# Channel-major projections of a hybrid decoder layer: TensorE in written order, small products in the middle of a later projection

## The chip, the cores and the metric

The kernel runs on one core of one Trainium2 chip. The time is the device time of one execution in microseconds (us), taken as the median of three executions. Lower is better.

## The reference, cut to what matters

One decoder layer over 2048 tokens of width 1024. The part that the change touches is the input projection `z = rms_norm(x) @ w_in` for the column groups that are kept with channels on the partitions, and what hangs on them:

```
z = rms_norm(x, norm_mix) @ w_in
# group A, gated linear recurrence
xc = causal_dwconv(xr, conv_w) + conv_b
r, i = sigmoid(xc @ w_gates[0] + b0), sigmoid(xc @ w_gates[1] + b1)      # block diagonal, 256 channels
a = exp(log_a);  b = sqrt(-expm1(2*log_a)) * (i * xc);  h = scan(a, b)
y_a = h * gelu(gate)
# group B, short convolution
y_b = bg * causal_dwconv(cg * xs)
# group D, compression of keys and of values: blocks of 32 tokens
kc = rms_norm(gelu(einsum('bnld,ldm->bnm', blocks, w1)) @ w2);  vc = the same without the norm
...
mixed = concat(rms_norm(y_a), rms_norm(y_b), rms_norm(y_c), rms_norm(y_d))
```

Attention, the output projection and the feed-forward part follow and are the larger part of the time; the change does not touch them.

## The kernel before

The normalised input lies in SBUF, transposed and split into a high and a low part (`xh`, `xl`, four blocks of 512 tokens). A projection takes one group of 128 weight columns and one block of 512 tokens: 8 slices of the depth, three matmuls each (`mm3`, lines 215 to 217), 24 matmuls into one PSUM tile `z` (pool of 5). There are 44 projections; the text numbers them 0 to 43 in the order of the list `steps`:

- 0 to 3: compression input (`cmp_block`)
- 4 to 7 and 8 to 11: recurrence input, the two halves of the channels (`lrux_block`)
- 12 to 19: the recurrence's gate, both halves in turn (`lrug_block`)
- 20 to 35: short convolution inputs; 36 to 43: its output gate (`scb_block`)

Each projection has a follow-up `fn`, which reads `z` and works on ScalarE (ACT), VectorE (DVE) and GpSimd (POOL). Some follow-ups need small matmuls of their own ("small products"), which are put on the list `later`:

- **gate products** (lines 677 and 679, eight pairs, `ms<-xc,wg`): the r and i gates of the recurrence for the block of one projection of 4 to 11. They need `xc`: two ACT instructions on `z` (667, 670), then three DVE instructions (672).
- Behind a pair of gate products comes a chain: sigmoid r and i, tanh (683 to 685, ACT), 1 + tanh (689, DVE), reciprocal (690, DVE), product (691, DVE), square root (692, ACT), product and scan (693, 694, DVE). Exp (686) is on ACT, a product (687) on POOL.
- **ones products** (line 505, eight times four): sums of squares for the output norm; the last half of the channels only.
- **compression products** (lines 560, 570, 582): 32 products with the compression weights `w1`, which SP loads in four pieces of 512 KB into the buffers of the projection weights, then two with `w2` and a transpose, with a gelu between.
- **decay products** (609, 610): two, for the forget gate's cumulative sum.

In the loop over `steps` the list is run (`drain`) after a projection is written and before its own follow-up; what a follow-up puts on the list is thus written behind the next projection. This is only the order in which the program is written: in this stage a scheduler of the framework orders every engine's queue by its own estimates. TensorE's rows therefore show small products inside later projections, where the scheduler found room. Each queue then runs strictly in its order. In the same stage the scheduler also places 16 `wo_prep` pieces: a load by SP, a cast on ACT (519), a subtraction on POOL (520), a store by SP; one buffer, so that each waits for the store of the one before.

Of the kernel before, what the change touches and what calls it, by code (L numbers as in the profile page):

```python
# [22 lines left out]
KD = D // 128  # L23
# [149 lines left out]
def kernel(ctx, tc, x, norm_mix, w_in, lru_conv_w, lru_conv_b, lru_w_gates, lru_b_gates,  # L173
# [40 lines left out]
    def mm3(ps, ah, al, bh, bl, start, stop):  # L214
        PE.matmul(ps, ah, bh, start=start, stop=False)  # L215
        PE.matmul(ps, ah, bl, start=False, stop=False)  # L216
        PE.matmul(ps, al, bh, start=False, stop=stop)  # L217
# [27 lines left out]
    with ExitStack() as A:  # L245
# [33 lines left out]
        with ExitStack() as A1:  # L279
# [154 lines left out]
            later = []  # L434
            for g, done in ((0, qk_done), (1, qk_done), (2, v_done)):
                for t in range(NT):
# [3 lines left out]
                    z = rows(g, t)  # L440
# [24 lines left out]
        with ExitStack() as A2:  # L465
# [6 lines left out]
            later = []  # L472
            full = {}
            state = {}

            def drain():
                todo = later[:]
                del later[:]
                for fn in todo:
                    fn()  # L480

            def newfull(name):
                full[name] = tm.tile([128, T], F32, name="full", tag="full")
# [2 lines left out]
            def proj(w, j):  # L486
                z = psz.tile([128, 512], F32, name="z")
                for k in range(KD):
                    mm3(z, w[0][:, k, :], w[1][:, k, :], xh[j][:, k], xl[j][:, k], k == 0, k == KD - 1)
                return z  # L490

# [3 lines left out]
            def y_out(g, c, j, y, sq):  # L495

                ACT.activation(sq, y, AF.Square)
                if c:
                    DVE.tensor_add(sq, sq, state["sq"])
                state["sq"] = sq  # L500

                def sums():
                    ms = psm.tile([128, 4, 4], F32, name="ms")
                    for i in range(4):
                        PE.matmul(ms[:, i], sq[:, i * 128:(i + 1) * 128], onec, start=True, stop=True)
                    dst = ssg[:, 4 * j:4 * j + 4, g, 0:1]
                    DVE.tensor_copy(dst, ms[:, :, 0:1])
                if c:
                    later.append(sums)
                k = 2 * g + c  # L510
                hl = tm.tile([128, 2, 512], F32R, name="hl")
                ACT.activation(hl[:, 0], y, AF.Copy, scale=col(R_ON + k))
                DVE.scalar_tensor_tensor(hl[:, 1], y, col(R_ON + k), f(hl[:, 0]), op0=OP.mult, op1=OP.subtract)
                (ACT if g else SP).dma_start(m_d[k, :, :, j * 512:(j + 1) * 512].rearrange("a p t -> p a t"), f(hl))
# [8 lines left out]
            def cmp_block(arg, z, j):  # L523
                if j == 0:
                    for i in range(2):
                        newfull(f"g{i}")
                for i in range(2):
                    zv = z[i * 64:(i + 1) * 64, :].rearrange("p (m e o) -> p e m o", e=8, o=2)
                    gv = full[f"g{i}"].rearrange("p (j n) -> p j n", n=128)
                    for o in range(2):  # L530
                        g = gv[o * 64:(o + 1) * 64]
                        m0 = 1 if j == 0 else 0
                        ACT.copy(g[:, 0:8, 32 * j:32 * j + 32], zv[:, :, :, o])
                        DVE.tensor_copy(g[:, 8:16, 32 * j - 1 + m0:32 * j + 31], zv[:, :, m0:, o])
                if j == 3:
                    later.append(compress)

            def gelu(dst, v, tmp):

# [7 lines left out]
            def compress():  # L547
                for i in range(2):
                    p0 = R_POS + 16 * i
                    gv = full[f"g{i}"].rearrange("p (j n) -> p j n", n=128)  # L550
                    DVE.tensor_copy(gv[:, :, 127], prm[:, p0:p0 + 16])
                    w2 = t1.tile([128, 64], F32, name="w2")
                    SP.dma_start(w2, nsa_cmp_w2[0, i])
                    hp = psk.tile([128, 512], F32, name="kps")
                    for hf in range(2):
                        w1 = wr.tile([128, KD, 128], F32, name="w1", tag="wraw")
                        SP.dma_start(w1, nsa_cmp_w1[0, i, 16 * hf:16 * hf + 16].rearrange(
                            "(j a) d m -> (a d) j m", a=2))
                        for jj in range(8):
                            PE.matmul(hp[:, :128], w1[:, jj, :], gv[:, 8 * hf + jj, :], start=jj + hf == 0,  # L560
                                      stop=jj + hf == 8)
                    hid = t1.tile([128, 128], F32, name="hid")
                    pc = t1.tile([128, 1], F32, name="pc")
                    DVE.tensor_copy(pc, hp[:, 127:128])
                    DVE.tensor_scalar(hid, hp[:, :128], pc, None, op0=OP.add)
                    hg = t1.tile([128, 128], F32, name="hg")
                    ht = t1.tile([128, 128], F32, name="ht")
                    gelu(hg, hid, ht)
                    op = psk.tile([128, 512], F32, name="kps")
                    PE.matmul(op[:, :64], hg, w2, start=True, stop=True)  # L570
                    if i:
                        ACT.copy(vcp[:, 0:64], op[:, :64])
                        DVE.tensor_sub(vcp[:, 64:128], op[:, :64], f(vcp[:, 0:64]))
                        continue
                    k2 = t1.tile([128, 2, 64], F32, name="k2")
                    ss = t1.tile([128, 3], F32, name="ss")
                    ACT.activation(k2[:, 0], op[:, :64], AF.Square, accum_out=ss[:, 0:1])
                    rstd(ss[:, 2:3], ss[:, 0:1], ss[:, 1:2], 1.0 / 64)
                    for a in range(2):
                        DVE.tensor_scalar(k2[:, a], op[:, :64], ss[:, 2:3], None, op0=OP.mult)  # L580
                    kt = psk.tile([128, 512], F32, name="kps")
                    PE.transpose(kt[:, :128], k2.rearrange("p a d -> p (a d)"), ident)
                    ktf = t1.tile([128, 128], F32, name="ktf")
                    kth = t1.tile([128, 128], F32R, name="kth")
                    DVE.tensor_scalar(ktf, kt[:, :128], col(R_KC), None, op0=OP.mult)
                    ACT.copy(kth, ktf)
                    DVE.memset(f(kcp), 0.0)
                    DVE.tensor_copy(kcp[0:64, 0:128], ktf[0:64])
                    DVE.tensor_sub(kcp[64:128, 0:128], ktf[64:128], f(kth[64:128]))

            def fox_decay():
# [16 lines left out]
                def sums():  # L608
# [6 lines left out]
                        DVE.tensor_tensor_scan(s[:, h, 1:NT], z[:, h, 1:NT], a[:, h, 0:NT - 1], 0.0, op0=OP.mult,  # L615
                                               op1=OP.add)
                    DVE.tensor_add(ccol, cp[:, 0:64].rearrange("p (h t) -> p h t", t=NT), s)
                later.append(sums)

            wg = t1.tile([128, 2, 2, 128], F32, name="wg")  # L620

# [133 lines left out]
            for ui, j in steps:  # L755
# [12 lines left out]
                        raws[ui + 3] = wload(wr, "wraw", ui + 3)  # L768
                if ui > 4 and wos:
                    wo_prep(*wos.pop(0))  # L770
                drain()
                fn(arg, z, j)
            drain()
            drain()
    if stop == "A":
        return dict(qk=qk_d, v=v_d, ccol=ccol, gates=gates, kcp=kcp, vcp=vcp)

# [1158 lines left out]
```

## Time and profile before

| what | value |
|---|---|
| median of 3 runs | 2719.72 us (2716.41 to 2719.79) |
| the profiled execution's own time | 2719.14 us |
| its span, first to last instruction | 2717.4 us |
| TensorE busy in the span | 2620.9 us (96%) |
| VectorE / ScalarE / GpSimd busy | 1751.0 (64%) / 1334.6 (49%) / 971.9 us (36%) |
| mean granted TensorE clock | 0.992 of full speed |

"Busy" counts an instruction from its start to its end. Matmuls are pipelined: they start about 0.23 us apart while each is shown as 0.39 us long, so a stage is timed here by starts. The channel-major projections run from about 279 to 582 us of the span.

### The profile page before, as it was taken

The page shows a single profiled execution, that of the slowest core. Times are in us where ns is not written, and L with a number is a line of the kernel's source. Part 1 is how long each engine was busy: PE and PEld are TensorE (multiplying, and loading weights), DVE is VectorE, ACT ScalarE, POOL GpSimd, SP SyncE. Part 2 cuts the span into 40 slices and gives each one's busy share as a digit, 9 for nine tenths or more (in the row PEclk, how much of TensorE's full clock was granted, in tenths as well). Part 3 has the DMA queues.
Part 4 walks back from the last instruction along what each step waited for, and adds up shares of the span by engine and source line. Part 5 has one row for each costly group of instructions (what it writes and reads, how often), then busy time and mean ns, then how long its engine had stood idle before and what let it go on. Part 6 is the DMA issues. An engine that isn't in the chain of part 4 may idle for free.

```text
span 2717.4 us, 39589 instructions
## 1 busy us (share of the span) xinstructions
PE 2620.9 (96%) x13483; PEld 2209.1 (81%) x13483; DVE 1751.0 (64%) x3823; ACT 1334.6 (49%) x2909; POOL 971.9 (36%) x1044
## 2 busy tenths in 40 slices
PE   7999988999988999999999999998999999999999
PEld 5899767889987988888877888887888888888887
DVE  5763487358899999886777666667666555333333
ACT  5431475149987888885444333234333323333331
POOL 1101125114566557750225433433431123224440
PEclk9999999999999999999999999999999999999999
DMA  5444313263432111046765544544543235664553
GB/s 166 121 112 115 118 59 134 77 188 94 110 81 76 50 46 40 25 156 218 247 209 163 175 147 145 169 155 159 178 144 119 75 117 179 211 194 128 184 182 104
DMA packets 314809, 364.73 MB, mean 134 GB/s; under 512 B 25504, under 2 KB 214127, under 8 KB 313839
## 3 DMA queue, kind: packets, MB, share of 16 engines
q1 hardware_dynamic: 312430, 358.02, 42.6%
q10 hardware_dynamic: 2176, 4.19, 0.4%
q8 instruction: 106, 1.74, 0.3%
q14 instruction: 97, 0.79, 0.1%
HBM read 240.24 MB, written 121.90 MB: 133 GB/s over the span
## 4 chain that ended last, share of the span: by engine, by line
PE 56%; DVE 3%; issue 1%; DMA 1%; ACT 1%; POOL 1%; SPq 0%; DVEq 0%; POOLq 0%; ACTq 0%
PE gu L1754 10%; PE gu L1755 10%; PE gu L1753 10%; PE d L1883 5%; PE d L1884 5%; PE d L1882 5%; PE px L215 2%; PE px L217 2%; PE px L216 2%; PE obank L1137 2%; PE tp L1115 1%; PE S L1045 1%; PE S L1046 1%; DMA xraw<-xf_d 1%; DVE P L1060 1%
## 5 line engine op out<-in xcount | busy, mean ns | idle before, releaser
L1753 PE MATMUL gu<-xh,g 128*128 128x512 f32 x1232 | 488.6, 397 | 7.9 <-DVE gq L1715 4.1
L1754 PE MATMUL gu<-xh,g 128*128 128x512 f32 x1232 | 488.6, 397 | 1.4 <-POOL g L1540 1.4
L1755 PE MATMUL gu<-xl,g 128*128 128x512 f32 x1232 | 487.9, 396 | 1.7 <-DVE xl L1663 1.7
L1540 POOL TENSOR_TENSOR g<-guraw,g 128x512 fp32r<-128x512 f32 x136 | 185.8, 1388 | 522.3 <-ACT g L1539 512.6
L1813 DVE TENSOR_TENSOR a<-araw,a 128x512 fp32r<-128x512 f32 x150 | 117.4, 784 | 268.6 <-ACT a L1812 268.6
L1753 PEld LDWEIGHTS gu<-xh,g 128*128 128x128 f32 x1232 | 233.1, 189 | 63.4 <-issue 5.0
L1755 PEld LDWEIGHTS gu<-xl,g 128*128 128x128 f32 x1232 | 233.2, 189 | 56.6 <-DVE xl L1663 2.5
L1754 PEld LDWEIGHTS gu<-xh,g 128*128 128x128 f32 x1232 | 233.0, 189 | 55.7 <-POOL g L1540 2.0
L925 POOL TENSOR_TENSOR pl<-pf,ph 128x512 fp32r<-128x512 f32 x179 | 230.3, 1294 | 111.7 <-ACT ph L911 48.6
L1082 ACT ACTIVATE P<-P,mn 128x1024 f32<-128x1024 f32 (+7 forms) x256 | 225.4, 888 | 20.8 <-DVE mn L1060 20.4
L1883 PE MATMUL d<-b,a 128*128 128x512 f32 x584 | 231.3, 396 | 0.0
L1884 PE MATMUL d<-b,a 128*128 128x512 f32 x584 | 231.2, 396 | 0.0
L1882 PE MATMUL d<-b,a 128*128 128x512 f32 x584 | 231.2, 396 | 0.0
L1812 ACT CAST a<-araw 128x512 fp32r<-128x512 f32 x150 | 93.0, 621 | 279.2 <-PE d L1884 265.7
L1137 PE MATMUL obank<-ph,v 128*128 128x256 f32 (+1 forms) x744 | 197.3, 292 | 3.6 <-ACT ob L962 3.1
L1115 PE MATMUL tp<-ident,P 128*128 128x128 f32 x1368 | 196.7, 274 | 1.2 <-DVE t L975 0.9
L1045 PE MATMUL S<-k,q 128*128 128x512 f32 (+2 forms) x432 | 174.4, 405 | 22.1 <-DVE mn L1060 18.9
L1137 PE MATMUL obank<-pl,v 128*128 128x256 f32 (+1 forms) x744 | 185.4, 283 | 4.2 <-POOL pl L925 2.1
L1115 PEld LDWEIGHTS tp<-ident,P 128*128 128x128 f32 x1368 | 160.0, 142 | 12.5 <-DVE t L975 1.2
L1824 POOL TENSOR_TENSOR b<-braw,b 128x512 fp32r<-128x512 f32 x73 | 102.3, 1414 | 182.7 <-ACT b L1823 181.1
L1046 PE MATMUL S<-k,q 128*128 128x512 f32 (+2 forms) x432 | 152.1, 353 | 0.0
L1539 ACT CAST g<-guraw 128x512 fp32r<-128x512 f32 x228 | 129.7, 617 | 42.6 <-DVE guraw L1610 35.0
(512 smaller groups left out, 6266.6 us busy)
## 6 DMA issues: line engine op xcount, KB each, us to landing
guraw<-in_w_gate_up_dram SPq DMA_DIRECT2D x88, 512.0 KB
araw<-hf_d SPq DMA_DIRECT2D x150, 256.0 KB
hf_d<-uq SPq DMA_DIRECT2D x88, 256.0 KB
q<-qk_d SPq DMA_DIRECT2D x80, 256.0 KB
hf_d<-gq SPq DMA_DIRECT2D x66, 256.0 KB
xt<-in_x_dram SPq DMA_DIRECT2D x32, 512.0 KB
xraw<-xf_d SPq DMA_DIRECT2D x24, 512.0 KB
dnraw<-in_w_down_dram SPq DMA_DIRECT2D x44, 256.0 KB
```

Of the source, the lines that this page charges most:

```text
L925: POOL.tensor_sub(tp["pl"], tp["pf"], f(tp["ph"]))
L1045: PE.matmul(dst, u["q"].tile[:, 0, qs], ks, start=True, stop=False)
L1082: ACT.activation(t, t, AF.Exp, bias=c["mn", a][:, n:n + 1], scale=-1.0, accum_out=c["sum"][:, x, a:a + 1])
L1115: PE.transpose(tp["tp"][:, si, a * 128:(a + 1) * 128], c["P", a, kt // 8][:, kt % 8 * 128:(kt % 8 + 1) * 128], ident)
L1137: PE.matmul(c["o"][:, cs], u["v"].tile[:, kt, :], tp[x][:, si, cs], start=gi == 0 and i == 0, stop=last and i == len(todo) - 1, skip_group ...
L1540: sub.tensor_sub(to[:, 1], src, f(to[:, 0]))
L1753: PE.matmul(p, wh[:, k], xh[:, k], start=j < 4 and k == 0, stop=False, skip_group_check=True)
L1754: PE.matmul(p, wl[:, k], xh[:, k], start=False, stop=False, skip_group_check=True)
L1755: PE.matmul(p, wh[:, k], xl[:, k], start=False, stop=k == HK - 1, skip_group_check=True)
L1882: PE.matmul(p, a[0][:, ts], w[0], start=first, stop=False, skip_group_check=True)
L1883: PE.matmul(p, a[0][:, ts], w[1], start=False, stop=False, skip_group_check=True)
L1884: PE.matmul(p, a[1][:, ts], w[0], start=False, stop=stop_, skip_group_check=True)
```

## The change

Three things change. TensorE's queue in this stage is no longer ordered by the scheduler: it runs in the order in which the program is written. `drain` is called inside a projection, after 12 of its 24 matmuls. And the list has a second level, `after`: what stands there moves to `later` at one drain and runs at the next. Ones products and decay products go to `after`; gate products stay in `later`. The compression becomes a generator that is advanced by one stage at each drain, with its loads of `w1` one stage ahead of the products.

```
@@ A2, before the projections
+            A2.enter_context(tc.manual_schedule(engines={mybir.EngineType.PE}))
+            after, stages = [], []
+
             def drain():
                 todo = later[:]
-                del later[:]
+                later[:] = after[:]
+                del after[:]
                 for fn in todo:
                     fn()
+                if stages:
+                    try:
+                        next(stages[0])
+                    except StopIteration:
+                        stages.pop(0)
@@ proj
                 for k in range(KD):
+                    if k == KD // 2:
+                        drain()
                     mm3(z, w[0][:, k, :], w[1][:, k, :], xh[j][:, k], xl[j][:, k], k == 0, k == KD - 1)
@@ y_out (ones products), fox_decay (decay products)
-                    later.append(sums)
+                    after.append(sums)
@@ cmp_block
-                    later.append(compress)
+                    stages.append(compress())
@@ compress: a yield before each group of eight w1 products, two before the w2 product, one before the transpose
+                        yield
                         for jj in range(8):
                             PE.matmul(hp[:, :128], w1[:, jj, :], gv[:, 8 * hf + jj, :], start=jj + hf == 0,
...
+                    yield
+                    yield
                     op = psk.tile([128, 512], F32, name="kps")
...
+                    yield
                     kt = psk.tile([128, 512], F32, name="kps")
@@ the loop over steps
-                drain()
                 fn(arg, z, j)
-            drain()
-            drain()
+            while later or after or stages:
+                drain()
```

TensorE's queue, projections 4 to 6 of the kernel before (`xh_127` and `xl_128` are the first block of tokens, `xh_129` the second, `xh_131` the third): the first pair of gate products, which belongs to projection 4, stands behind the whole of projection 5, with a compression product between.

```order
L215 MATMUL z<-xh_129,wh_2548 128x512
L216 MATMUL z<-xl_130,wh_2548 128x512
L217 MATMUL z<-xh_129,wl_2550 128x512
L677 MATMUL ms<-xc,wg 128x512
L570 MATMUL kps<-w_2919,hg 128x64
L679 MATMUL ms<-xc,wg 128x512
L215 MATMUL z<-xh_131,wh_2548 128x512
```

The same pair in the changed kernel (its lines 692 and 694 are 677 and 679 of before, 572 is 560): it stands in the middle of projection 5, with the first eight `w1` products behind it.

```order
L215 MATMUL z<-xh_129,wh_2548 128x512
L216 MATMUL z<-xl_130,wh_2548 128x512
L217 MATMUL z<-xh_129,wl_2550 128x512
L692 MATMUL ms<-xc,wg 128x512
L694 MATMUL ms<-xc,wg 128x512
L572 MATMUL kps<-full,w_2912 128x128 x8
L215 MATMUL z<-xh_129,wh_2548 128x512
```

What moved: every pair of gate products now stands half a projection behind the projection that it belongs to. Counted through the whole queue, the eight pairs stood in the middle or at the start of projections 6, 7, 9, 9, 12, 12, 15 and 15 (the last one after 367 of the 1056 projection matmuls); now they stand in the middle of 5 to 12 (the last one after 300). The compression products stand in 5, 6, 8, 9, 10, 11 and 13, the ones products in 16, 18, 20, 22, 40 and 42 and, the last two groups, at the end.

VectorE's queue late in the recurrence inputs, before: two blocks' chains (689 to 694) are worked in pairs, with the `xc` instructions (672) of two later projections behind one another.

```order
L691 TENSOR_TENSOR it<-it,lrc 128x512
L689 TENSOR_SCALAR lrc<-it 128x512
L690 RECIPROCAL lrc<-lrc 128x512
L693 TENSOR_TENSOR it<-it 128x512
L691 TENSOR_TENSOR it<-it,lrc 128x512
L694 SCALAR_TENSOR_TENSOR full<-lr,full,it 128x512
L672 SCALAR_TENSOR_TENSOR xc<-xr,prm,xc 128x512 x4
L693 TENSOR_TENSOR it<-it 128x512
```

The same queue of the changed kernel at the seventh and eighth block (704 to 709 are 689 to 694 of before, 687 is 672, 576 to 577 are 564 to 565, the start of the compression's second gelu):

```order
L704 TENSOR_SCALAR lrc<-it 128x512
L705 RECIPROCAL lrc<-lrc 128x512
L687 SCALAR_TENSOR_TENSOR xc<-xr,prm,xc 128x512
L706 TENSOR_TENSOR it<-it,lrc 128x512
L687 SCALAR_TENSOR_TENSOR xc<-xr,prm,xc 128x512
L681 COPY xr<-xr 128x3
L687 SCALAR_TENSOR_TENSOR xc<-xr,prm,xc 128x512
L708 TENSOR_TENSOR it<-it 128x512
L709 SCALAR_TENSOR_TENSOR full<-lr,it 128x512
L576 COPY pc<-kps 128x1
L709 SCALAR_TENSOR_TENSOR full<-lr,full,it 128x512
L577 TENSOR_SCALAR hid<-kps,pc 128x128
```

What moved: one block's chain at a time, and the `xc` of the next block stands behind the reciprocal of the block before it; two scans and the compression's first instructions stand ahead of the next chain.

GpSimd's queue in the recurrence inputs, one piece of the difference (702 is 687 of before, 531 is 520, the subtraction of `wo_prep`):

```order
-L687 TENSOR_TENSOR it<-it,xc 128x512 x2
-L520 TENSOR_TENSOR wo<-wo 128x512
-L687 TENSOR_TENSOR it<-it,xc 128x512 x2
+L702 TENSOR_TENSOR it<-it,xc 128x512
+L531 TENSOR_TENSOR wo<-wo 128x512
+L702 TENSOR_TENSOR it<-it,xc 128x512
+L531 TENSOR_TENSOR wo<-wo 128x512 x2
+L702 TENSOR_TENSOR it<-it,xc 128x512
```

What moved: one or two `wo` subtractions now stand between every two blocks of the recurrence; before, three ran in this stretch.

## Rows read from the trace of the kernel before

**Rows 1.** Windows: from, to, length, busy of PE, PEld, DVE, ACT, POOL
```profile
311.00:404.00 93.00, 82.19 (x354) 61.09 (x354) 69.51 (x87) 65.11 (x87) 20.43 (x14) 0.98 0.26 83
```

**Rows 2.** Waits of PE, 278 to 582 us: total us, times, longest
```profile
PE ms L505 <- DVE gt L499: 4.9, 3, 2.0
PE ms L677 <- issue: 4.1, 1, 4.1
PE kps L560 <- DMA w<-in_nsa_cmp_w_dram: 2.8, 3, 1.9
PE kps L609 <- DVE fe L602: 2.8, 1, 2.8
PE kps L570 <- DVE hg L545: 1.9, 1, 1.9
PE ms L677 <- DVE xc L672: 1.9, 1, 1.9
PE ms L505 <- DVE tt L719: 1.6, 1, 1.6
PE z L215 <- DVE gg L700: 1.3, 1, 1.3
```

**Rows 3.** Timeline of PE, undisturbed projections: start, length (us); 399 matmuls later
```profile
464.16 0.39 PE L217 MATMUL z<-xh,wl 128*128 128x512 f32 x1
...
554.64 0.39 PE L217 MATMUL z<-xh,wl 128*128 128x512 f32 x1
```

**Rows 4.** Timeline of PE behind the decay products; 10 matmuls later
```profile
294.01 0.63 PE L216 MATMUL z<-xl,wh 128*128 128x512 f32 x1
...
298.27 0.63 PE L217 MATMUL z<-xh,wl 128*128 128x512 f32 x1
```

**Rows 5.** Timeline: projection 4's end, its xc, first and last gate product
```profile
312.18 0.39 PE L217 MATMUL z<-xh,wl 128*128 128x512 f32 x1
...
313.91 2.33 DVE L672 SCALAR_TENSOR_TENSOR xc<-xr,prm,xc 128x512 f32<-128x512 f32 x3 [0.51 <-ACT xc L670]
...
324.35 1.02 PE L677 MATMUL ms<-xc,wg 128*128 128x512 f32 x2
...
402.84 1.02 PE L677 MATMUL ms<-xc,wg 128*128 128x512 f32 x2
```

**Rows 6.** Timeline: instructions of the chain, from several blocks
```profile
399.63 1.12 PE L677 MATMUL ms<-xc,wg 128*128 128x512 f32 x2 [1.89 <-DVE xc L672]
402.30 0.71 ACT L685 ACTIVATE it<-lr,lcoef 128x512 f32<-128x512 f32 x1
...
381.25 1.00 DVE L689 TENSOR_SCALAR lrc<-it 128x512 f32<-128x512 f32 x1 [2.45 <-ACT it L685]
382.29 3.35 DVE L690 RECIPROCAL lrc<-lrc 128x512 f32<-128x512 f32 x1
385.68 0.69 DVE L691 TENSOR_TENSOR it<-it,lrc 128x512 f32<-128x512 f32 x1
...
350.08 1.40 DVE L672 SCALAR_TENSOR_TENSOR xc<-xr,prm,xc 128x512 f32<-128x512 f32 x2
```

**Rows 7.** Groups of instructions in 311 to 404 us: count, busy us, mean ns
```profile
L692 ACT ACT_TABLE_LOAD x6 | 7.7, 1283 | 0.1
...
L694 DVE TENSOR_TENSOR_SCAN full<-lr,full,it 128x512 f32<-128x512 f32 x4 | 5.1, 1272 | 0.0
```

**Rows 8.** Timeline: a POOL subtraction and a DVE product beside it
```profile
372.62 2.78 POOL L271 TENSOR_TENSOR wl<-wraw,wh 128x1024 fp32r<-128x1024 f32 x1
...
373.13 2.82 DVE L693 TENSOR_TENSOR it<-it 128x512 f32<-128x512 f32 x1
```

**Rows 9.** Timeline: a gate product behind the longest stall, and its tanh
```profile
376.71 1.40 PE L677 MATMUL ms<-xc,wg 128*128 128x512 f32 x2 [4.13 <-issue]
...
380.50 0.71 ACT L685 ACTIVATE it<-lr,lcoef 128x512 f32<-128x512 f32 x1
```

**Rows 10.** Timeline: the first of the last two groups of ones products
```profile
578.43 0.95 PE L505 MATMUL ms<-onec,sqy 128*128 128x4 f32 x8
```

More of the change, by code (lines that the diff above doesn't have):

```diff
@@ L617, in sums @@
                     DVE.tensor_add(ccol, cp[:, 0:64].rearrange("p (h t) -> p h t", t=NT), s)
-                later.append(sums)
+                after.append(sums)
             wg = t1.tile([128, 2, 2, 128], F32, name="wg")
@@ L770 @@
                     wo_prep(*wos.pop(0))
+                fn(arg, z, j)
+            while later or after or stages:
                 drain()
-                fn(arg, z, j)
-            drain()
-            drain()
     if stop == "A":
```

## The prediction

> **What bounds the kernel now.** I looked first at the busy table: TensorE is busy 96% of the span, so a change of its order can only win back its stalls and the time at half clock, stage by stage. The stage is the channel-major projections, 279 to 582 us. There are 44 x 24 = 1056 projection matmuls; undisturbed they start 90.48 / 399 = 0.2268 us apart [rows 3], so they need 239.5 of the 303 us. The rest is small products, waits and half clock. The table of waits [rows 2] shows which: eight entries, together 21.3 us; another, 1.5 us at the very end, stays in place. That is what could be won, plus some half clock: behind the 2.8 us wait for the decay products matmuls start 4.26 / 10 = 0.426 us apart [rows 4], which is 1.2 of the 2.4 GHz.
>
> Then I asked who is late. In 311 to 404 us, the recurrence inputs, TensorE was busy 82 of 93 us, VectorE 70 and ScalarE 65 [rows 1]. The last gate product started at 402.84, the first at 324.35 [rows 5]: seven blocks in 78.5 us, 11.2 each, while a projection with its pair of gate products needs only 24 x 0.2268 + 1.3 = 6.7 us of TensorE. So the pace here is that of the chain on VectorE and ScalarE; TensorE filled the time with later projections and had issued 367 matmuls when the last pair came. The changed order allows it 300.
>
> **The change, part by part.**
>
> *The start.* The decay products come a projection and a half later, where their input is long there. This saves the wait of 2.8, 10 x (0.426 - 0.227) = 2.0 us of half clock and some 0.7 around it: 5.5 us. Projection 4's last matmul thus starts at 312.18 - 5.5 = 306.7. Its `xc` was ready 313.91 + 2.33 - 312.18 = 4.1 us after that start [rows 5], so 310.8; half a projection is 2.7 us, so TensorE waits 1.4 us there. Before, this pair stood behind the whole next projection and the first compression products, at 324.35: the chain begins 13.5 us sooner.
>
> *The chain, per block.* After the start of a gate product its tanh ends 402.30 + 0.71 - 399.63 = 3.4 us later; then 1.00 (add), 3.35 (reciprocal), and, in the new order of VectorE, one `xc` instruction, the product (0.69) and two more `xc` instructions (1.40 for two, so 0.70 for one) [rows 6], with 0.2 for a copy and hand-overs. The next gate product waits for the last of these: 3.4 + 1.0 + 3.35 + 0.7 + 0.69 + 1.4 + 0.2 = 10.7 us. TensorE cannot shorten this, and it can no longer run past: it has 6.7 us of work per block, 8.5 with eight `w1` products, so it idles 2 to 4 us in each. Seven blocks: 74.9 us.
>
> *What stands in the chain's way.* (a) The compression's VectorE and ScalarE work now lies inside five of the seven intervals. The queues show ahead of the next link: gelu pieces of 0.2 to 0.4 us, another table load for the tanh and one for the square root (1.28 each), one scan in front of `xc` (1.27) and, at the seventh block, two [rows 7]. Some of it hides beside the reciprocal. I take 9 us; all hidden would be 0, all in line about 12. (b) A `wo` subtraction on GpSimd now falls between every two blocks, just when VectorE has its products to do. Beside a GpSimd subtraction of 2.78 us a VectorE product of 0.69 us ended after 2.82, 0.55 us after GpSimd's end [rows 6, 8]: it was held. A subtraction of 128x512 is half that long, so up to 1.4 per block; I take 4 us for seven blocks, with 0 and 7 as bounds. The Trainium skill (SBUF — State Buffer, "Who interferes with whom") has it as an exclusive lock: a VectorE instruction with two SBUF inputs blocks for the whole GpSimd instruction. By that rule the upper bound would be the better value; the rows agree where the two start together, but not every block will.
>
> (c) Half clock. Behind the 4.1 us stall a gate product took 1.40 instead of 1.12 us, and its tanh ended 380.50 + 0.71 - 376.71 = 4.5 us after its start instead of 3.4 [rows 6, 9]. The stalls of 2.8 and 4.1 us were followed by half clock, those of 1.9 us were not [rows 2, 4, 9]. By the sums above, idling is 2 to 3 us in three of the seven intervals and over 4 in the others. I take 1.1 us in three or four of them, 4 us; 0 and 8 are the bounds.
>
> *The last gate product* then starts at 310.8 + 74.9 + 9 + 4 + 4 = 402.7, which is where it was (402.84); but 67 matmuls fewer are done, 15.2 us.
>
> *What is behind it.* The pair takes 1.3 us. Then come 756 x 0.2268 = 171.5 us of projections, six groups of ones products at about 1.0 [rows 10], 0.7 for the last compression product and restarts: 402.7 + 1.3 + 171.5 + 6.0 + 0.7 = 582.2 for the start of the last two groups. Before, that start was at 578.4 [rows 10]: 402.84 + 1.3 + 689 x 0.2268 = 156.3, + 6.0, + the waits of 4.9 + 1.6 + 1.3 [rows 2], and the remaining 4 us restarts and half clock. Those 7.8 us of waits go, and the 4 with them, because a group now stands two projections behind its `later` piece, 10.9 us, where it stood one behind. I leave 1.2 us of them (bounds 0 and 6.5), since the weight casts of projections 20 and 24 and the bias table now stand in front of the last blocks' work on ScalarE and GpSimd. Sum: 582.2 + 1.2 - 578.4 = +5.0.
>
> The other engines' rows outside the stage and what follows it are unchanged; the tail of the stage too. The waits for `w1` (2.8) vanish, because each piece is asked for a stage ahead, hidden behind at least 10 us of chain against some 4 us of loading; they are in the sum by the first gate's time.
>
> On the profiled execution's 2719.14 us this gives 2724.1; I say **2724**. It is 0.16% above the median of 2719.72, so inside the 0.2% (5.4 us) that I take as what a measurement can tell from no change.
>
> **The rivals.**
>
> 1. *Faster: the pieces hide.* Compression, `wo` and clock cost next to nothing, because the reciprocal (3.35) and the table loads leave holes for them. Then the last gate product starts near 310.8 + 74.9 + 3 = 388.7, and the sum becomes 5.0 - 14 = -9: 2710. For it: VectorE was busy only 70 of 93 us [rows 1]. Against: the queues are strict, and the pieces stand in front of the link, not beside it.
>
> 2. *Clearly slower: every gate at half clock.* Each of the seven pairs costs 1.1 us, (a) and (b) are at their upper ends: + 4 + 3 + 3, and 2 us of half clock behind the last pair: 5.0 + 12 = +17, 2736. The table [rows 2] speaks for it as far as idle stretches over 2.8 us are concerned. It decides against the kernel when the last gate product starts later than about 403.1. The Trainium skill (TensorE: Matmul & The Clock Gate, "Why this matters for your kernels") speaks against this change: it advises against idle gaps between bursts of matmuls, because the clock falls back to half. By it nearly all of the seven would be slow; here stalls of 1.9 us were not.
>
> 3. *Nothing changes,* because this stage's pace is VectorE's and ScalarE's whatever TensorE does: what is won at the start and at the ones products is lost at the gates. This is my forecast but for its size; the sum leans by 5 us to the slow side.
>
> 4. *The ones products still wait.* If ScalarE's casts hold the gate blocks' gelu up, the 6.5 us of waits stay: 2729. A part of the slower case.
>
> **How the numbers follow.** Within 0.2%: 0.43, the likeliest, around 2724 (the forecast, with rival 3). Slower by more: 0.39 (0.29 for rival 2 and for any two of (a) to (c) above what I took, 0.10 for rival 4). Faster by more: 0.18 (rival 1). The range reaches to both: from 2710 (rival 1) to 2735 (nearly rival 2); I leave 1 in 10 on either side. The likeliest case's own range is 2715 to 2725.
>
> **What would show it.** After: gate products waiting for `xc` in nearly all eight places, together 25 to 35 us, where it was 6 [rows 2]; no waits for the decay products, `w1` and the ones products; first gate product near 311, last near 403; intervals of 11 to 15 us; more windows at half clock between 311 and 404. The prediction is wrong if the last gate product starts before 392 (the pieces hide) or after 410 (the lock, the clock or a late `wo` load that holds ScalarE's queue cost more than I took), or if ones products wait over 3 us in all.

## Result and profile after

The changed kernel takes **2741.53 us** (median of 5, 2738.64 to 2746.84) against 2719.72 us (median of 5): ratio **1.0079, 95% interval 1.0069 to 1.009**, slower by some 21.5 us. The forecast was 2724 and the range 2710 to 2735; the time lies above it. The profiled execution took 2738.64 us, 19.5 more than the profiled one of before, with a span of 2736.9. In the changed kernel's file the lines of the stage are 11 to 15 higher: the gate products are 692 and 694, the `xc` instructions 687, add, reciprocal, product 704 to 706, the scan 709, the ones products 516, the `w1` products 572, the `wo` cast and subtraction 530 and 531.

First TensorE's waits from 278 to 606 us, to set beside [rows 2] (total us, times, longest):

```profile
PE ms L692 <- DVE xc L687: 27.2, 7, 7.7
PE ms L692 <- issue: 6.5, 1, 6.5
PE ms L516 <- DVE gt L510: 4.9, 2, 3.5
PE ms L516 <- DVE sqy L510: 1.5, 1, 1.5
PE z L217 <- POOL wl L271: 0.8, 1, 0.8
```

All eight gate pairs wait, 33.7 us in all. The waits for the decay products, for `w1` and for the compression's gelu (`hg`) are gone, and those of the ones products fell from 6.5 to 4.9. Without the 1.5 us at the end, which stayed, TensorE stalls 39.4 us where it stalled 21.3.

Then the places, from the timeline of TensorE (start, duration, and in brackets the wait ahead):

```profile
312.81 1.12 PE L692 MATMUL ms<-xc,wg 128*128 128x512 f32 x2 [2.82 <-DVE xc L687]
...
383.98 1.10 PE L692 MATMUL ms<-xc,wg 128*128 128x512 f32 x2 [3.39 <-DVE xc L687]
...
394.78 1.10 PE L692 MATMUL ms<-xc,wg 128*128 128x512 f32 x2 [1.57 <-DVE xc L687]
...
411.70 2.05 PE L692 MATMUL ms<-xc,wg 128*128 128x512 f32 x2 [7.71 <-DVE xc L687]
413.54 1.91 PE L694 MATMUL ms<-xc,wg 128*128 128x512 f32 x2
...
479.52 1.03 PE L516 MATMUL ms<-onec,gt 128*128 128x4 f32 x8 [3.52 <-DVE gt L510]
```

The eight pairs start at 312.81, 326.30, 341.13, 355.36, 370.90, 383.98, 394.78 and 411.70: intervals of 13.5, 14.8, 14.2, 15.5, 13.1, 10.8 and 16.9, 98.9 us together (before 78.5, [rows 5]). The pairs at 341, 355, 371 and 412 ran at half clock, 2.02 to 2.05 instead of 1.10 us for the two matmuls of a first product; at 313 and 326 only the second product was slow (1.83 and 1.63 instead of 1.02), and the pairs at 384 and 395 were not slow at all. The last two groups of ones products start at 600.88 instead of 578.43 [rows 10]; the layer's later parts give 3 us back.

Who kept the pairs waiting? The waits of VectorE in the same stretch, and two places of its timeline:

```profile
DVE lrc L704 <- ACT it L700: 17.7, 7, 4.8
...
DVE full L709 <- PE kps L572: 8.3, 2, 5.0
```

```profile
326.07 0.68 DVE L708 TENSOR_TENSOR it<-it 128x512 f32<-128x512 f32 x1
331.73 1.23 DVE L709 TENSOR_TENSOR_SCAN full<-lr,it 128x512 f32<-128x512 f32 x1 [4.97 <-PE kps L572]
...
387.31 1.00 DVE L704 TENSOR_SCALAR lrc<-it 128x512 f32<-128x512 f32 x1 [2.87 <-ACT it L700]
388.34 3.35 DVE L705 RECIPROCAL lrc<-lrc 128x512 f32<-128x512 f32 x1
391.83 0.75 DVE L687 SCALAR_TENSOR_TENSOR xc<-xr,prm,xc 128x512 f32<-128x512 f32 x1
...
398.55 1.22 DVE L709 TENSOR_TENSOR_SCAN full<-lr,it 128x512 f32<-128x512 f32 x1 [3.32 <-PE kps L572]
```

VectorE itself was waiting: at seven blocks for the tanh that follows the pair, and at two places, with the *first scan of each half of the channels*, for `w1` products. The two buffers of the tag `full` explain the second: `h0` and `h1` get the buffers of `g0` and `g1`, so the first scan into them cannot start until the last `w1` product has read `g`, and the stages put that product behind pair two (331.7) and pair seven (398.6).

ScalarE's timeline (start, duration, wait ahead):

```profile
313.74 0.62 ACT L530 CAST wo<-wo 128x512 fp32r<-128x512 f32 x1 [3.35 <-DMA wo<-in_w_out_dram]
...
390.52 0.59 ACT L682 COPY xr<-z 128x512 f32<-128x512 f32 x1 [0.70 <-PE z L217]
391.01 0.79 ACT L685 ACTIVATE xc<-z,prm 128x512 f32<-128x512 f32 x1
...
395.44 0.62 ACT L530 CAST wo<-wo 128x512 fp32r<-128x512 f32 x1 [1.60 <-DMA wo<-in_w_out_dram]
396.08 1.28 ACT L698 ACT_TABLE_LOAD   x1
399.81 0.69 ACT L698 ACTIVATE lr<-ms,prm 128x512 f32<-128x512 f32 x1 [2.44 <-DVE pc L576]
```

Casts of `wo` stand in front of the sigmoid and wait there for their own load, and at 399.81 the sigmoid waits until the held-up scans release a buffer of `lr`. The interval from 383.98 to 394.78, with neither, is the bare one: 10.8 us.

No engine was full. Busy times from 311 to 385 us, of the changed kernel and, for comparison, of the best kernel below (`sums_later_still`):

```profile
311.00:385.00 74.00, 50.67 (x178) 34.84 (x179) 52.31 (x63) 50.61 (x66) 19.57 (x13) 0.86 0.28 97
```

```profile
311.00:385.00 74.00, 67.60 (x290) 49.95 (x290) 66.48 (x81) 63.77 (x84) 20.07 (x13) 0.98 0.30 93
```

(Columns: length, then busy time of TensorE, its weight loads, VectorE, ScalarE and GpSimd, the granted clock, DMA share and GB/s.) VectorE was busy 52 of 74 us, and can be for 66.

### The profile page after: what moved, and what is told of

Its sections match the earlier page's. It is cut to its first block, busy times and chain, and to the rows that moved or that the text cites. A ratio compares the mean times of both kernels' runs of the same rounds, so it can differ in the third digit from the quotient of the medians.

```text
span 2736.9 us, 39586 instructions
## 1 busy us (share of the span) xinstructions
PE 2623.2 (96%) x13483; PEld 2208.3 (81%) x13483; DVE 1750.4 (64%) x3823; ACT 1336.5 (49%) x2908; POOL 975.2 (36%) x1044
## 4 chain that ended last, share of the span: by engine, by line
PE 53%; DVE 4%; issue 2%; ACT 1%; DMA 1%; POOL 1%; DVEq 0%; SPq 0%; POOLq 0%; ACTq 0%
PE gu L1769 9%; PE gu L1768 9%; PE gu L1767 9%; PE d L1898 5%; PE d L1896 5%; PE d L1897 5%; PE px L215 2%; PE px L217 2%; PE px L216 2%; PE obank L1151 1%; PE tp L1129 1%; DMA xraw<-xf_d 1%; PE S L1059 1%; DVE P L1074 1%; PE S L1060 1%
## 5 line engine op out<-in xcount | busy, mean ns | idle before, releaser
L1129 PEld LDWEIGHTS tp<-ident,P 128*128 128x128 f32 x1368 | 159.2, 141 | 12.5 <-DVE t L989 1.2
```

Of the source, the lines that this page charges most:

```text
L1129: PE.transpose(tp["tp"][:, si, a * 128:(a + 1) * 128], c["P", a, kt // 8][:, kt % 8 * 128:(kt % 8 + 1) * 128], ident)
```

## The experiments

Two theories stood at the start. *Held buffer*: the first scans wait for `w1` products behind a later pair. *Distance*: VectorE and ScalarE set the pace, as the prediction had it, and what counts is how many matmuls TensorE has done by the last pair, 5.4 us for each projection. The first four runs brought a third. *Loop*: the pair stands half a projection behind its own, so the second half of the next projection waits behind it; the latencies pair, `z`, `xc`, pair (and pair, tanh, reciprocal, `xc`) then lie in series, block after block, though no engine is full.

The kernel before was measured again beside each group of experiments (medians of 2720.5 to 2723.0 us), so small differences are told by ratios to it; the changed kernel's is 1.0079. One hundredth of a ratio is 27 us. In the lines of a run the line numbers differ by a few from the changed kernel's.

**w1_before_pairs.** In `compress`, ahead of the `w1` products:

```
-                        yield
```

> The changed kernel, only without the pause ahead of each of the four groups of w1 products: groups one and two then stand on TensorE ahead of the first gate pair, three and four behind the third pair, instead of behind pairs one, two, six and seven. Theory of the held buffer: g0 and g1 share two buffers with h0 and h1, so the first scan of each half waits until the w1 products that read g are done, and these stand behind the pair of the next-but-one block; VectorE stood idle 4.97 and 3.32 us for that. Then the second interval between pairs falls from 14.8 to 11 to 12 us and the last from 16.9 to 12 to 14, both scans wait for no w1 product, and the time falls by 5 to 8 us, to 2733 to 2737. Rival, the chain is as long with or without it (casts of wo, compression's pieces, half clock): the idle time goes elsewhere, the intervals sum to 96 or more as before (98.9), 2739 to 2742.

Measured: 2753.94 us, ratio 1.0114 (1.0099 to 1.0129). Neither: no scan waits for a `w1` product any more, but the `w1` loads were asked for at the moment of use, and TensorE waited for them.

```profile
PE kps L571 <- DMA w<-in_nsa_cmp_w_dram: 13.5, 3, 5.6
```

It tells that the pause is worth having (the changed kernel has no such wait), and nothing of what the buffer costs.

**pairs_one_later, pairs_two_later.** In `lrux_block`:

```
-                later.append(fin)
+                after.append(fin)
```

(for two later, a further list behind `after`).

> The changed kernel, only with the gate pairs placed one projection later on TensorE (one and a half behind their own instead of a half). Theory of the distance: the stage's pace is the chain's, so TensorE passes each pair when the chain lets it, and what counts is how many matmuls it has done by the last pair; 24 more are 5.4 us. The held buffer goes too, since the second group of w1 products then stands right behind the first pair. 5.4 and 5 to 8 together: 2728 to 2731; waits ahead of pairs stay at 6 to 8 places. Rival, the distance is worth nothing because the buffers of xc and of z hold TensorE back at the next place: the last pair starts later by what was gained, 2734 to 2738 from the buffer alone.

> The changed kernel, only with the gate pairs two projections later (two and a half behind their own). Theory of the distance: another 5.4 us, 2722 to 2726, near the kernel before, whose last pair stood behind 15.8 projections where this one has 15.25 and the changed kernel 13.25. Rival, buffers hold TensorE back: no better than pairs_one_later.

Measured: one later 2715.56 us, ratio **0.9976** (0.9965 to 0.9986); two later 2734.59, 1.0048 (1.0031 to 1.0065). One later won 28 us, where I had expected 10 to 13 (5.4 for the distance, the rest for the buffer), and no pair waits for `xc` any more. Its timeline of TensorE, and its waits:

```profile
317.24 1.02 PE L692 MATMUL ms<-xc,wg 128*128 128x512 f32 x2
...
326.21 1.02 PE L692 MATMUL ms<-xc,wg 128*128 128x512 f32 x2
...
333.42 1.02 PE L692 MATMUL ms<-xc,wg 128*128 128x512 f32 x2
...
383.86 1.07 PE L692 MATMUL ms<-xc,wg 128*128 128x512 f32 x2
```

```profile
PE ms L516 <- DVE gt L510: 12.8, 2, 8.7
PE kps L597 <- DVE k L594: 7.9, 1, 7.9
```

Intervals of 9.0 and 7.2 us are TensorE's own work: 24 matmuls (5.4), a pair (1.8), with or without eight `w1` products (1.7). The first two intervals took 28.3 us in the changed kernel and take 16.2 here; all seven take 66.6 (one of them 17.9, with the 7.9 us wait at the transpose) where they took 98.9, with the same work. That refutes 10.7 us per block, 74.9 for seven, as the pace of VectorE and ScalarE: each of them is now busy 60 of 67 us (317 to 384). It is what led to the loop. The scans' wait for `w1` fell with it, from 8.3 to 1.0 us, so the 28 us are not the loop's alone. What is left waits at the next place, the transpose and the ones products. My expectation had the sign, not the size, because I still thought of distance. Two later is slower than one later: it takes no more waits away (the pairs had none) and starts the last pair 12.5 us later, at 396.35 instead of 383.86; on ScalarE its sigmoids and square root then stand between the pieces of the gate blocks' gelu, and the ones products, left in their place, wait:

```profile
PE ms L518 <- DVE gt L512: 24.4, 3, 19.1
```

**scheduler_orders.** The line that sets the program order is left out, everything else stays:

```
-            A2.enter_context(tc.manual_schedule(engines={mybir.EngineType.PE}))
```

> The changed kernel, only without the line that puts TensorE in program order: the scheduler places its instructions again, the drain in the middle of a projection, the later sums and the compression in stages stay. By the order of instructions its pairs stand behind 7.5, 9.2, 9.6, 12.3, 12.5, 14.2 and 15.75 projections and all four w1 groups ahead of the first scan that needs their buffer. Theory of the distance: 2.5 projections or 13.6 us are won back, and the held buffer's 5 to 8, 2718 to 2724. Rival, the staging lengthens the chain whoever orders TensorE: 2733 or more.

Measured: 2718.63 us, ratio 0.9988 (0.9977 to 0.9999). The staging costs nothing by itself; the order does. By the order of instructions the scheduler puts the last pair some 2.5 projections further back, and at the pairs TensorE waits 10.9 us instead of 33.7.

**drain_at_end, stages_before_pairs, and both (end_and_stages_first).** In `proj`, and in `drain`:

```
-                    if k == KD // 2:
-                        drain()
                     mm3(...)
+                drain()
```

```
-                for fn in todo:
-                    fn()
                 if stages:
...
+                for fn in todo:
+                    fn()
```

> The changed kernel, only with the small products placed behind the last matmul of the second projection instead of in its middle, half a projection (2.7 us of matmuls) later. Theory of the loop: in the changed kernel the second half of a projection stands behind the pair of the block before, so its z, then its xc (4.6 us from z to the pair), then its own pair can only come after it: pair, half a projection, xc, pair again, 10 to 11 us a block at least, and TensorE waits at each. With the pair behind the whole projection z is done before the pair, xc runs beside, and the loop is broken: intervals of 7 to 9 us, few waits for xc, the waits move to the ones products; 2712 to 2722, close to pairs_one_later. Rival, distance only: 2.7 us are won and no more, intervals sum to 95 or more, 2737 to 2740.

> The changed kernel, only with each compression stage issued ahead of the gate pair at the same place instead of behind it; its loads keep their distance of a stage. Theory of the held buffer: the first scan of each half no longer waits for w1 products (4.97 and 3.32 us of VectorE idle), the second interval falls from 14.8 to 11 to 12 and the last from 16.9 to 13 or 14; 2734 to 2737. Rival, the loop alone sets the pace and VectorE's idle time lay beside it: 2739 to 2742.

> Both edits of drain_at_end and stages_before_pairs together. If the loop and the held buffer are two causes, their gains (17 and 8 us) mostly add up: 2716 to 2720, no first scan waiting for w1 products, second interval under 12 where drain_at_end has 16.3. Rival: with the pair behind the whole projection the buffer is no longer what VectorE waits for, and the gain is what drain_at_end has: 2722 to 2727.

Measured: 2724.47 us, ratio 1.0013 (1.0004 to 1.0023); 2733.77, 1.0047 (1.0032 to 1.0062); both 2715.19, 0.9982 (0.9972 to 0.9991). Against 1.0079 the first wins 0.0066 (18 us), the second 0.0032 (9 us), both 0.0097 (26 us): **the gains of the two edits add up**. With the drain at the end only 2.7 us of matmuls more are done by the last pair; the seven intervals shrink from 98.9 to 85.9 us, 12.3 in the mean. That is less than the theory of the loop had (7 to 9 us each, 2712 to 2722).

For the held buffer the stages first are the cleaner test: the second interval falls from 14.8 to 11.7 and the last from 16.9 to 13.9, as expected, while of the other two that had `w1` products behind their pair the first gains 0.4 (13.5 to 13.1) and the sixth loses 2.6 (10.8 to 13.4). Merely moving these products out from behind a pair is thus not what wins. All seven sum to 91.0 (315.14 to 406.13):

```profile
315.14 1.12 PE L692 MATMUL ms<-xc,wg 128*128 128x512 f32 x2 [0.88 <-DVE xc L687]
...
406.13 1.10 PE L692 MATMUL ms<-xc,wg 128*128 128x512 f32 x2 [4.12 <-DVE xc L687]
```

VectorE's waits (278 to 606 us) do not divide as cleanly as the gains. With the stages first the scan's wait for `w1` is gone and that for the tanh stays; with the drain at the end the wait for the tanh is halved, but the scan's wait falls too, from 8.3 to 0.3; with both the tanh's is 5.8:

```profile
DVE lrc L704 <- ACT it L700: 19.4, 8, 4.8
```

```profile
DVE lrc L703 <- ACT it L699: 9.5, 6, 2.9
...
DVE full L708 <- PE kps L571: 0.3, 1, 0.3
```

```profile
DVE lrc L703 <- ACT it L699: 5.8, 6, 1.9
```

So the edits do not stand for one cause each: what the stages first win on top of the drain at the end (9 us) cannot be the scan's wait, since only 0.3 us of it were left. That the loop and the held buffer are two causes that add up is argued, not shown. What the drain at the end does to the loop shows in the first blocks. With it, `z` of the next block is complete ahead of the pair, and its `xc` stands in front of the block's own add:

```profile
315.76 2.31 DVE L686 SCALAR_TENSOR_TENSOR xc<-xr,prm,xc 128x512 f32<-128x512 f32 x3
318.86 1.01 DVE L703 TENSOR_SCALAR lrc<-it 128x512 f32<-128x512 f32 x1 [0.78 <-ACT it L699]
```

Single long waits stay (8.81 us at 378.5; with both, 12.63 at 353.2), where the scheduler has put an `xc` behind other links of earlier blocks: with a distance of one projection some of the loop is left.

**wo_after_the_stage.** Each `wo` load depends on the projection of its own step:

```
+                DVE.tensor_copy(f(wo[:, 1, 0:1]), z[:, 0:1])
                 SP.dma_start(f(wo[:, 1]), ...)
```

> The changed kernel, only with each of the 16 wo loads held until the projection of its own step has a result (a copy of one column per load on VectorE), so that no cast on ScalarE and no subtraction on GpSimd lies between gate pairs. If terms (a) and (b) of the prediction and the casts that wait for their load are what makes an interval of 10.8 into 14.1 us: the seven intervals sum to 85 to 92 instead of 98.9, no VectorE product takes over 1.3 us there, 2730 to 2737. Rival, loop and held buffer: intervals sum to 95 or more, 2738 to 2742, or above if the casts now hold the gate blocks up.

Measured: 2747.37 us, ratio 1.0098 (1.0082 to 1.0113). Inside the stage it did what the first half of its expectation says: the intervals sum to 90.9 us (401.01 - 310.12), 8.0 less, and GpSimd's busy time from 311 to 385 us is 10.1 instead of 19.6. But the time rose: the casts now lie among the short convolution, where projections wait for their `z` buffer.

```profile
PE z L215 <- ACT full L730: 6.4, 4, 2.1
PE z L215 <- DVE tt L741: 3.3, 3, 2.2
PE z L215 <- DVE yb L750: 0.8, 1, 0.8
```

So 8 us of the stage are the `wo` work's. What that work must cost elsewhere is not shown: the added copies themselves stand in VectorE's queue there and wait for the one `wo` buffer, and ScalarE's copies of `z` wait for them in turn (31.1 us; both from 420 to 606 us).

```profile
DVE wo L529 <- DMA wo_d<-wo: 78.4, 14, 9.0
```

**filled_waits.** Ahead of a pair, into its own PSUM tile, twelve matmuls whose result is overwritten:

```
+                    for _ in range(12):
+                        PE.matmul(pr, xh[j][:, 0, 0:128], xh[j][:, 0], start=True, stop=True)
                     PE.matmul(pr, wg[:, c, 0, :], xc, start=True, stop=True)
```

> The changed kernel with twelve more matmuls of 128x512 ahead of each gate pair, on operands that are long there, written into the pair's own PSUM tile and overwritten by it (the output is the same): 2.7 us of work where TensorE waits 1.6 to 7.7 us, so that the pair is not behind an idle stretch. Theory of the clock, term (c) as a cost of this size: pairs at the full clock, 1.0 to 1.1 us for two instead of 2.05, no z at half clock behind them, 1.1 us and up to another for what waits for the late z at five places: 2733 to 2737. Rival: the granted clock is not what sets the pace, since a pair that ends sooner finds ScalarE behind a table load or a cast, and where the wait is shorter than 2.7 us the matmuls add to it: 2740 to 2746.

Measured: 2738.46 us, ratio 1.0059 (1.0044 to 1.0074); the interval overlaps the changed kernel's, so whether anything was won is not sure, and the median lies between the two expectations. The clock did change:

```profile
339.09 1.12 PE L694 MATMUL ms<-xc,wg 128*128 128x512 f32 x2 [1.30 <-DVE xc L687]
...
352.77 2.07 PE L694 MATMUL ms<-xc,wg 128*128 128x512 f32 x2 [3.49 <-DVE xc L687]
```

Five pairs came at the full clock (behind 0 to 1.4 us of idle left), three at half (behind 2.9 to 4.9); in the changed kernel two pairs had both products at the full clock. The intervals sum to 97.5, only 1.4 less, and the first of the last two groups of ones products starts at 600.92, where it starts at 600.88 in the changed kernel. The fillers also cost something themselves: where the wait was shorter than their 2.7 us, the interval grew (the sixth, from 10.8 to 11.8). So half clock at the three pairs that were helped is worth some 2.4 us; what it costs at the three others was not tested.

**program_order_alone.** This is the kernel before with only the line that sets the order:

```
+            A2.enter_context(tc.manual_schedule(engines={mybir.EngineType.PE}))
```

> The kernel before with only TensorE in program order: the drain stays behind each projection, the compression in one piece, each group of sums one projection behind. Its pairs stand a whole projection behind their own, so the loop is absent; but the compression stands in one piece between two projections, with two loads, two gelus and a transpose that TensorE has to wait for in place: 25 to 40 us of waits there, of which the stage's slack takes back some. I expect 2735 to 2755, so that program order by itself costs and the stages of the change win part of it back. Rival: program order by itself is what cost the 22 us whatever the stages do: 2760 or more with gates waiting in all eight places; or it costs nothing, 2715 to 2725.

Measured: 2757.81 us, ratio 1.0138 (1.0121 to 1.0155): just above my range, under the rival's. The compression's waits are where I put them, 20.6 us and so less than I thought, with two long ones for `xc` besides:

```profile
PE ms L679 <- DVE xc L674: 21.2, 2, 11.1
PE kps L562 <- DMA w<-in_nsa_cmp_w_dram: 11.1, 3, 5.0
...
PE kps L572 <- DVE hg L547: 5.7, 2, 3.2
PE kps L584 <- DVE k L582: 3.3, 1, 3.3
```

So the other parts of the change win back 16 us of what the program order costs.

**pairs_later_products_early, sums_later_still.** Both start from `pairs_one_later`. In the first, the four groups of `w1` products come in four projections one after the other, then the two small compression products and the transpose with three and two drains between them, and all ones products stand one projection later. In the second, the ones products of the gate blocks stand later still (the last line; the first has `more[1]` there).

```
+                    hids.append(hid)
+                for i in range(2):
+                    hid = hids[i]
...
                     gelu(hg, hid, ht)
-                    yield
-                    yield
+                    for _ in range(3):
+                        yield
...
-                    yield
+                    for _ in range(2):
+                        yield
...
-                    after.append(sums)
+                    more[[2, 2, 2, 3][j] if g == 0 else 1].append(sums)
```

> pairs_one_later, with the four groups of w1 products one projection after the other and the two small compression products and the transpose behind the stage (3 and 2 projections between them), and the sums of squares one projection later still. If the waits of pairs_one_later (12.8 for sums of squares, 7.9 for the transpose) only come from where these stand: they fall under 6 in all and the time to 2700 to 2708. Rival, VectorE and ScalarE set the pace by now and the waits come back at the next place: 2710 to 2718.

> pairs_later_products_early with the sums of squares of the four gate blocks two projections later than the changed kernel has them (three for the last). If its 10.6 us of waits there come from the place alone: under 3, and 2702 to 2706. Rival, VectorE (60 of 73 us busy or more) sets the pace: the waits go to the z buffers or the next sums and the time stays within 4 us of 2712.

Measured: 2711.86 us, ratio 0.9962 (0.995 to 0.9973), and **2705.15, 0.9938 (0.9923 to 0.9953)**. The first landed in the rival's range: it moved the waits more than it removed them (10.6 for the ones products, 4.5 for `xc`). The second came out as expected, so the place of the ones products was the reason and not the pace of VectorE; it has these waits left:

```profile
PE ms L699 <- DVE xc L694: 4.5, 3, 2.2
PE z L217 <- POOL wl L271: 3.2, 1, 3.2
PE kps L604 <- DVE k L600: 1.9, 1, 1.9
PE ms L518 <- DVE sqy L512: 1.5, 1, 1.5
```

It beats both kernels, with the same idea as the change and other distances.

## Why the prediction was wrong

Two terms of the sum failed. "What stands in the chain's way" was 24.0 us instead of 17: the scans' wait for a buffer that `w1` products hold, 7.9 us, was put at nothing, and the `wo` work at half of its 8.0. The stretch behind the last gate product was 8.5 us longer than forecast. The chain's number came out, but it was taken for an engine's pace. On the last two groups of ones products the change came out 17.5 us later than the sum (600.88 against 582.2 + 1.2). By its steps:

- *The start: right but for 2.0 us.* The decay products waited for nothing (298.45); the first pair started at 312.81 instead of 310.8, since a cast of `wo`, which had itself waited 2.1 us for GpSimd, and the copies into `g` behind it stood ahead of `xr` on ScalarE. Without the `wo` work the pair started at 310.12 (`wo_after_the_stage`).
- *The chain per block, 10.7 us: the number right, the meaning wrong.* The bare interval is 10.8. But I took it for the pace of VectorE and ScalarE, from which TensorE could only fall back. It is a loop of latencies that the change itself makes; `pairs_one_later` ran six of its seven intervals in 7.2 to 9.0 us, and the kernel 28 us faster. From that step came rival 3, "nothing changes", and with it the weight on the middle. The profile of before had the hint: VectorE busy 70 and ScalarE 65 of 93 us [rows 1] is no bound.
- *What stands in the chain's way, (a) to (c), 17 us: mis-sized, 24.0* (98.9 - 74.9). Missed altogether was the held buffer, 7.9 us of the intervals (98.9 against 91.0 in `stages_before_pairs`; 6.1 of them in the two intervals where the scans waited). The `wo` work of (b) and the casts that wait for their load took 8.0 (`wo_after_the_stage`), where I had 4 and named a late `wo` load only as a risk. The clock (c), where I had 4, is not measured as a whole: the fillers took half clock from three pairs and won 1.4 net, some 2.4 without what they cost themselves. An estimate from the trace puts the whole near 5: behind the pairs at 341, 355 and 371 the tanh ended 5.0, 4.7 and 5.1 us after the start, behind the one at 384 after 3.3. What is left for compression's pieces (a), 3 to 6 us where I had 9, no run priced by itself, and the parts need not add exactly.
- *Behind the last gate product: 189.2 us instead of 180.7.* The pair ran at half clock (2.76 instead of 1.3; a pair at the full clock takes 1.8, 394.78 to 396.57, so the 1.3 was too small in itself), the matmuls behind it lost 1.3, the ones products waited 4.9 instead of 1.2, half clock followed (1.4), and a projection waited 0.8 for its weights. Two of the prediction's own signs of being wrong came here: ones products that wait over 3 us, and a last pair after 410.

Rival 2 gave 2736 and decided from 403.1 on; the last pair came at 411.70, so the side was its, but its reason is borne out only in part: half of its 12 us were the clock's, with each of the first seven pairs at half clock, where three were wholly and two in part; and it had no term for the held buffer. The rule of the Trainium skill behind it (TensorE: Matmul & The Clock Gate, "Why this matters for your kernels": no idle gaps between bursts of matmuls) is borne out in the clock: the four first products behind the longest waits came at 2.02 to 2.05 us for two matmuls, and with the waits filled five came at 1.02 to 1.13. It warned of the right place, though the gaps, 33.7 us of waits, cost more than the clock in them.

On (b), the lock. In the changed kernel a copy of three columns shows it best; the view is the timeline of all engines:

```profile
323.71 1.76 POOL L531 TENSOR_TENSOR wo<-wo 128x512 fp32r<-128x512 f32 x1 [5.42 <-ACT wo L530]
324.27 1.23 DVE L681 COPY xr<-xr 128x3 f32<-128x3 f32 x1
```

It takes 0.16 us elsewhere (393.76 us) and ended here at the same time as GpSimd's subtraction (325.50 and 325.47). The Trainium skill (SBUF — State Buffer, "Who interferes with whom") has copies among what can take the shared port pair and then block wholly; the trace agrees.

What stays open: the drain at the end moves the compression's products, takes away the scans' wait and lets the scheduler order VectorE otherwise, so its 18 us are not the loop's alone, and the share of TensorE's leg of the loop (`z` behind the pair) and of VectorE's (`xc` behind the reciprocal) is not split. In the bare interval both end together: the reciprocal at 391.69, `xc` on ScalarE at 391.80.

## What to carry to other kernels

Where the engine in front is put in program order, a small product that depends on the result of an earlier step, by way of other engines, needs distance to that step, or the latencies of all engines add up in a loop: half a step made one here, a whole step left single long waits, one and a half left no wait at these products; the sign is that TensorE, VectorE and ScalarE are all partly idle and wait for one another in turn. Before calling a chain an engine's pace, compare that engine's busy time with the stretch. And look for buffers that a moved reader still holds: here a stage delayed on TensorE stopped a scan on VectorE that has nothing to do with it but the buffer.

## What had not been expected of the hardware

A copy of 128x3 elements on VectorE can take 1.23 us instead of 0.16 beside a GpSimd subtraction, so even tiny instructions in a chain are exposed. And twelve matmuls per pair whose result nobody reads, 96 in all, did not lengthen the kernel (2738.46 against 2741.53 us): most of them lay inside waits, and where a wait was shorter than they are, an interval grew by 1.0 us.
